# A fused three-layer forward pass on one core: one input tile's layout, one buffer and several places in the order changed

## The chip, the cores and the metric

The kernel runs on one core of one Trainium2 chip. The metric is the device time of one execution in microseconds (us); lower is better.

## What is computed

The input x has 256 rows of 1024 columns, the two memories (mem and mem_2) as many. All is fp32. Cut to what matters:

```python
def first_block(x, mem, ...):
    for l in range(2):
        a = hybrid_mixer(rms_norm(x, pre_mix_g[l]), ...)
        x = x + rms_norm(a, post_mix_g[l])
        c = memory_cross_attention(rms_norm(x, pre_xattn_g[l]), rms_norm(mem, mem_g[l]), ...)
        x = x + rms_norm(c, post_xattn_g[l])
        hdn = jnp.square(jax.nn.relu(rms_norm(x, pre_mlp_g[l]) @ w_up[l]))
        x = x + rms_norm(hdn @ w_down[l], post_mlp_g[l])
    return x

def second_block(x, mem, ...):
    z = rms_norm_2(x, norm_mix_g) @ w_in
    u, v, q, kv, gl = jnp.split(z, splits, axis=-1)
    a = spatial_gating_unit(gelu(u), gelu(v), ...)
    b = nsa_attention(q, kv, gl, ...)
    mixed = concatenate([rms_norm_2(a, mix_out_g[0]), rms_norm_2(b, mix_out_g[1])])
    x = x + mixed @ w_out
    x = x + memory_cross_attention_2(rms_norm_2(x, norm_mem_g), mem, ...)
    return x + square(relu(rms_norm_2(x, norm_ffn_g) @ w_ff1)) @ w_ff2
```

`hybrid_mixer` is one projection into a low-rank query and key-value part (8 heads, rotary part of 32) and a dilated part (8 heads of 64, three window patterns, a position bias), two attentions and one output projection. `memory_cross_attention` has 4 heads of 256. `nsa_attention` joins three branches by a sigmoid gate for each head: a softmax over all earlier keys (the selected blocks are all blocks here, and the window is longer than the input, so both are causal attentions), and one over 15 compressed keys and values. These come from blocks of 32 rows, flattened to 2048 columns, through gelu(flat @ w1 + b1) @ w2 + b2. `memory_cross_attention_2` has 4 heads of 128 with a norm on queries and keys. The MLPs are 4096 wide.

## The kernel before

The 256 rows are two tiles of 128 (t = 0, 1). A fp32 product is made from parts: every operand is split into a hi and a lo part, and three matmuls are summed: hi by hi, hi by lo, lo by hi (`mm3`, L181 to 184).

Weights come in pieces of 512 KB through SP's queue into a ring of four raw buffers, and are split into the ring `whl` of eight: ScalarE writes the hi part (L170, or L174 where a gain is multiplied in), VectorE the lo part (L171, L175). The PSUM banks are four `ps`, two `tp` (mostly transposes), `pf0` and `pf1`.

A normalised and transposed input, `hT`, holds both parts in one tile of shape [128, 2, kt, T] (L308, `new_hT`), part outside, 128-row block of the columns (kt) inside, T = 256. The memory's tile `mem` is made likewise (L507, `load_mem`); hT, the attentions' output `oT` and the like share two buffers under the tag h16. `projA` has the input as the stationary operand and the weights as the moving one. `projS` turns that round, and uses that both parts lie in one tile:

```python
PE.matmul(banks[c], hi[:, cs], xT[2][:, :, k], start=k == 0, stop=False, skip_group_check=True)
PE.matmul(banks[c][:, 0], lo[:, cs], xT[0][:, k], start=False, stop=k == KT - 1, skip_group_check=True)
```

The first (L248) moves 512 columns, hi and lo of the input's block k; the second (L249) 256. `projS` serves the low-rank and dilated projections of the mixer, the memory's keys and, as `up`, the first half of the MLPs.

A scheduler decides the order on each engine from the order in the program and a priority: instructions on VectorE, ScalarE and GpSimd are given one that is 600 earlier (AHEAD, L41). What is to stand inside a projection is handed to it as `at={k: f}`: f is issued ahead of step k. Transposes on TensorE (L278, L405, L628, L826, L902, L1390) are placed so. Such a step needs an operand that VectorE or ScalarE has evacuated from PSUM, and its own result is evacuated by the two in turn.

The places that the change touches:

- Start: twelve matmuls on a constant (L469), and then the gains' transposes.
- `mixer` (L647): key projection, with the transposes of the low-rank inputs (`transp_split(cns[t], ...)` into `cT`) at steps 2 and 5; the rotary key rows `krs`; then the second dilated projection, with the memory's transposes (`memory([0])`) at step 6 and `memory([1])` behind it.
- `mem_attention` (L834), for `cross` (layers 0 and 1, four heads of 256) and `cross2`. A query projection returns a function that transposes it (`turn`). `scores`, softmax and `values` run per row tile; the exps `e` are transposed (L405, result `eT`) and multiplied with the memory's values (L859); L851 are the scores. At its end stand `values(0)`, `turn1()`, `scores(1)`.
- `mlp` (L889): `up01` makes the first two of eight column blocks, with the transposes of the block before (`turn`, L902, of `relu`) at step 3; `down(0)` has the last of them at step 3 too.
- `mixer2` (L1023): projections for u and v with the second row tile's input transposes (`first`) at step 4; pooled and separate keys and values; the first compression layer, `hidden(kd, qs)`, in batches of 16 matmuls of 32 rows by 256 (L1083, kd = 0 for keys, 1 for values), whose weights come through the raw ring; then the query projections with smaller steps inside them. `gates` is a sigmoid from exp. `ckeys0`, `ckeys` make the compressed keys and values, `cscores` their scores. The table `MIX2` (L44) says what is issued ahead of which group of the causal attentions; `mk0`, `mk1` are the second memory's key projection for one row tile each.
- `cross2` (L1367): the query's norms (`head_ms`, four squares with a sum on ScalarE) are read from PSUM in `query`.

## Time and profile before

| | |
|---|---|
| median of three runs | 1209.34 us (1208.45 to 1210.66) |
| profiled execution | 1207.37 us |
| its span, first to last instruction | 1205.3 us |
| TensorE busy (share of the span) | 1178.3 us (98%) |
| VectorE, ScalarE, GpSimd busy | 810.4, 716.5, 83.6 us |
| mean granted TensorE clock | 0.999 |
| share of the chain that ended last | TensorE 76%, DMA 7%, VectorE 7%, ScalarE 6% |
| moved by DMA | 213.12 MB, 177 GB/s on average |

In the rows below PE is TensorE, DVE VectorE, ACT ScalarE, POOL GpSimd, SP the engine whose queue issues the loads. `out<-in` are the tiles an instruction writes and reads, then partitions x elements; xN is a count. A matmul's recorded time overlaps that of the next one, so the price of one is the distance from its start to the next start. The granted clock is the share of TensorE's full clock that the chip allowed. "Idle before <-X" is how long an engine stood ahead of an instruction, and what ended that.

### The profile page before, as it was taken

How to read it: one execution, taken by the hardware profiler on the slowest of the kernel's cores; microseconds unless marked ns; L12 is line 12 of the kernel's file. 1: busy time of each engine (PE TensorE's matmuls, PEld its weight loads, DVE VectorE, ACT ScalarE, POOL GpSimd, SP SyncE). 2: the span in 40 equal slices, each digit the busy share in tenths (PEclk: the TensorE clock that was granted, in tenths of full speed). 3: DMA queues.
4: the chain of work that ended last, by engine and by line, in shares of the span. 5: the costliest groups of instructions: out<-in, count | busy, mean ns of one | idle time of the engine just before them, and what ended most of it. 6: DMA issues, size and time to landing. Idle time of an engine off the chain costs nothing.

```text
span 1205.3 us, 17865 instructions
## 1 busy us (share of the span) xinstructions
PE 1178.3 (98%) x6430; PEld 981.8 (81%) x6430; DVE 810.4 (67%) x1583; ACT 716.5 (59%) x1492; POOL 83.6 (7%) x161
## 2 busy tenths in 40 slices
PE   8999999999999999999999999999999999999998
PEld 6788888888888898778888788887877787888887
DVE  6777766576676676766757676667658657766653
ACT  7766655565565575755648565557676557655551
POOL 1100010110000020000202000002022011000000
PEclk9999999999999999999999999999999999999999
DMA  8856265176656386454625756655663224666560
GB/s 263 296 183 223 98 216 196 59 233 194 191 180 197 116 265 196 148 190 157 208 90 193 240 179 200 195 178 166 198 207 106 88 88 138 211 191 188 183 192 35
DMA packets 92182, 213.12 MB, mean 177 GB/s; under 512 B 7285, under 2 KB 21055, under 8 KB 91327
## 3 DMA queue, kind: packets, MB, share of 16 engines
q1 hardware_dynamic: 91666, 211.62, 54.6%
q8 instruction: 50, 0.82, 0.3%
q10 hardware_dynamic: 428, 0.37, 0.1%
q14 instruction: 38, 0.30, 0.1%
HBM read 205.66 MB, written 6.30 MB: 176 GB/s over the span
## 4 chain that ended last, share of the span: by engine, by line
PE 76%; DMA 7%; DVE 7%; ACT 6%; issue 2%; POOL 1%; SPq 0%; ACTq 0%; POOLq 0%; DVEq 0%
PE ps L184 11%; PE ps L182 11%; PE ps L183 11%; PE pf L248 8%; PE tp L248 6%; PE pf L249 4%; PE pf L182 4%; PE pf L184 4%; PE pf L183 4%; DVE whl L175 3%; PE tp L249 3%; ACT whl L174 2%; DMA raw<-in_w_in_dram 2%; PE ps L446 2%; PE ps L851 1%
## 5 line engine op out<-in xcount | busy, mean ns | idle before, releaser
L175 DVE SCALAR_TENSOR_TENSOR whl<-raw,gT,whl 128x512 fp32r<-128x512 f32 (+5 forms) x416 | 295.0, 750 | 99.1 <-ACT whl L174 98.7
L174 ACT ACTIVATE whl<-raw,gT 128x512 fp32r<-128x512 f32 (+5 forms) x416 | 277.0, 717 | 131.0 <-issue 59.8
L171 DVE TENSOR_TENSOR whl<-raw,whl 128x512 fp32r<-128x512 f32 x264 | 170.3, 686 | 79.6 <-ACT whl L170 79.1
L170 ACT ACTIVATE whl<-raw 128x512 fp32r<-128x512 f32 x264 | 153.7, 628 | 110.7 <-issue 77.7
L182 PE MATMUL ps<-whl,mid 128*128 128x512 f32 x384 | 150.5, 392 | 0.0
L184 PE MATMUL ps<-whl,mid 128*128 128x512 f32 x384 | 149.8, 390 | 0.0
L183 PE MATMUL ps<-whl,mid 128*128 128x512 f32 x384 | 149.6, 390 | 0.0
L248 PE MATMUL pf<-hT,whl 128*128 128x512 f32 x352 | 132.6, 399 | 0.0
L248 PE MATMUL tp<-hT,whl 128*128 128x512 f32 x288 | 107.9, 398 | 0.0
L249 PE MATMUL pf<-hT,whl 128*128 128x256 f32 x352 | 98.8, 281 | 0.0
L182 PE MATMUL ps<-whl,hT 128*128 128x512 f32 (+4 forms) x240 | 85.6, 356 | 0.0
L184 PEld LDWEIGHTS ps<-whl,mid 128*128 128x128 f32 x384 | 72.1, 188 | 15.6
L184 PE MATMUL ps<-whl,hT 128*128 128x512 f32 (+4 forms) x240 | 84.1, 350 | 0.4 <-DVE hT L135 0.4
L182 PEld LDWEIGHTS ps<-whl,mid 128*128 128x128 f32 x384 | 72.1, 188 | 15.1
L183 PE MATMUL ps<-whl,hT 128*128 128x512 f32 (+4 forms) x240 | 84.1, 350 | 0.0
L183 PEld LDWEIGHTS ps<-whl,mid 128*128 128x128 f32 x384 | 72.1, 188 | 14.5
L249 PE MATMUL tp<-hT,whl 128*128 128x256 f32 x288 | 80.9, 281 | 0.0
L248 PEld LDWEIGHTS pf<-hT,whl 128*128 128x128 f32 x352 | 66.1, 188 | 16.2 <-DVE qkd L135 0.3
L249 PEld LDWEIGHTS pf<-hT,whl 128*128 128x128 f32 x352 | 66.5, 189 | 0.0
L248 PEld LDWEIGHTS tp<-hT,whl 128*128 128x128 f32 x288 | 54.1, 188 | 13.2 <-DVE mem L135 0.2
L182 PE MATMUL ps<-whl,oT 128*128 128x512 f32 x152 | 60.8, 400 | 0.0
L184 PE MATMUL ps<-whl,oT 128*128 128x512 f32 x152 | 59.7, 393 | 0.0
(323 smaller groups left out, 2261.9 us busy)
## 6 DMA issues: line engine op xcount, KB each, us to landing
raw<-in_w_up_dram SPq DMA_DIRECT2D x64, 512.0 KB
raw<-in_w_down_dram SPq DMA_DIRECT2D x64, 512.0 KB
raw<-in_w_ff_dram SPq DMA_DIRECT2D x64, 512.0 KB
raw<-in_w_in_dram SPq DMA_DIRECT2D x40, 512.0 KB
raw<-in_w_xk_dram SPq DMA_DIRECT2D x16, 512.0 KB
raw<-in_w_xv_dram SPq DMA_DIRECT2D x16, 512.0 KB
raw<-in_w_mix_out_dram SPq DMA_DIRECT2D x16, 512.0 KB
raw<-in_w_xq_dram SPq DMA_DIRECT2D x16, 512.0 KB
```

What stands on the lines that cost most here:

```text
L170: nc.scalar.activation(hl[:, 0, c:d], raw[:, c:d], AF.Copy)
L171: nc.vector.tensor_tensor(out=hl[:, 1, c:d], in0=raw[:, c:d], in1=hl[:, 0, c:d].bitcast(F32), op=ALU.subtract)
L174: nc.scalar.activation(hi[:, i], r[:, i], AF.Copy, scale=g[i])
L175: nc.vector.scalar_tensor_tensor(lo[:, i], r[:, i], g[i], hi[:, i].bitcast(F32), ALU.mult, ALU.subtract)
L182: PE.matmul(o, sh, mh, start=start, stop=False, skip_group_check=True)
L183: PE.matmul(o, sh, ml, start=False, stop=False, skip_group_check=True)
L184: PE.matmul(o, sl, mh, start=False, stop=stop, skip_group_check=True)
L248: PE.matmul(banks[c], hi[:, cs], xT[2][:, :, k], start=k == 0, stop=False, skip_group_check=True)
L249: PE.matmul(banks[c][:, 0], lo[:, cs], xT[0][:, k], start=False, stop=k == KT - 1, skip_group_check=True)
L446: PE.matmul(cell["o"][j * 64:j * 64 + 64, h // 2], vf(h, kb), pp[j][i][kb] if bias is None else pp[j][i][kb][:, ::-1], start=begin and i = ...
L851: PE.matmul(s[:, i], qT[:, c, tq], kT[:, c], start=(i == 0 and k == 0), stop=k == nkt - 1, skip_group_check=True)
```

## The change

1. hT and mem get the shape [128, kt, 2, T]: for each block k the two parts lie side by side, and L248 moves one run of 512 columns.
2. Fifteen matmuls in place of twelve at the start.
3. First and second mixer layer: cT's transposes at steps 1 and 6. In layer 0 `rows`, `memory([0])` and `memory([1])` go into steps 2, 5 and 7 of the second dilated projection, and `krs` is made behind that.
4. `turn1()` ahead of `values(0)`.
5. MLP: `turn` at step 5 in `up01`, at step 6 in `down(0)`.
6. Second mixer: `first` at step 6; the keys' compression weights in an h16 buffer (`w1`), loaded at the block's start, and their four quarters of `hidden(0)` inside the last pooled projection; `gates` ordered behind the last gelu; compressed keys at steps 1 and 7 of the second query projection, scores inside `mk0`, values inside `mk1`.
7. `cross2`: the query's norms are read from its SBUF copy, and made in `turn`; the last MLP's first weights are converted behind the copy of the last turned query.

```diff
-                PE.matmul(banks[c], hi[:, cs], xT[2][:, :, k], start=k == 0, stop=False, skip_group_check=True)
+                PE.matmul(banks[c], hi[:, cs], xT[2][:, k], start=k == 0, stop=False, skip_group_check=True)
...
-        h = h16p.tile([128, 2, kt, T], F32R, tag="h16", name=nm)
-        return (h[:, 0], h[:, 1], h)
+        h = h16p.tile([128, kt, 2, T], F32R, tag="h16", name=nm)
+        return (h[:, :, 0], h[:, :, 1], h)
...
-    for _ in range(12):
+    for _ in range(15):
...
-        memT[2] = memp.tile([128, 2, 8, T], F32R, tag="mem", name="mem")
-        memT[0], memT[1] = memT[2][:, 0], memT[2][:, 1]
+        memT[2] = memp.tile([128, 8, 2, T], F32R, tag="mem", name="mem")
+        memT[0], memT[1] = memT[2][:, :, 0], memT[2][:, :, 1]
...
-                                    at={2 + 3 * t: lambda t=t: transp_split(cns[t], t, cT, 0, 5) for t in range(2)})):
+                                    at={1 + 5 * t: lambda t=t: transp_split(cns[t], t, cT, 0, 5) for t in range(2)})):
...
-            rows()
             memory = load_mem(I["mem"])
+        wd = load_all(w, 8, 1184, 512, gp)
+        for i, b in enumerate(projS(wd, hT, 4, ["ps", "ps", "pf0", "pf1"], at={2: rows, 5: lambda: memory([0]), 7: lambda: memory([1])} if l == 0 else {})):
+            halves(qkd[:, 1, i], b)
...
-        wd = load_all(w, 8, 1184, 512, gp)
-        for i, b in enumerate(projS(wd, hT, 4, ["ps", "ps", "pf0", "pf1"], at={6: lambda: memory([0])} if l == 0 else {})):
-            halves(qkd[:, 1, i], b)
...
-            memory([1])
...
+        turn1()
         values(0)
-        turn1()
         scores(1)
...
-            ws = [load_all(w_up, 8, j * 512, 512, g) for j in range(2)]
+            if held[0] is None:
+                ws = [load_all(w_up, 8, j * 512, 512, g) for j in range(2)]
+            else:
+                with tc.issue_after(held[0].ins):
+                    ws = [load_all(w_up, 8, j * 512, 512, g) for j in range(2)]
...
-                    at = {} if turn is None else {3: turn}
+                    at = {} if turn is None else {5: turn}
...
-            last = down(j, mids, {} if j else {3: turn})
+            last = down(j, mids, {} if j else {6: turn})
...
-            uvb = [projA(wuv[i], hT, t, [(0, 512)], at={4: first} if i == 1 and t == 0 else {})[0] for i in range(2)]
+            uvb = [projA(wuv[i], hT, t, [(0, 512)], at={6: first} if i == 1 and t == 0 else {})[0] for i in range(2)]
...
+        w1 = h16p.tile([128, 16, 256], F32, tag="h16", name="w1")
+        for q4 in range(4):
+            nc.sync.dma_start(w1[:, q4 * 4:q4 * 4 + 4],
+                              I["cmp_w1_2"][0, 0, q4 * 512:q4 * 512 + 512, :].rearrange("(m p) n -> p m n", p=128))
...
-            wib[t], = projA(ww, hT, t, [(0, 280)])
+            wib[t], = projA(ww, hT, t, [(0, 280)], at={2 * q + 1: lambda q=q: hidden(0, [q]) for q in range(4)} if t else {})
             keys(t)
-            if t == 0:
-                hidden(0)
...
-            for t in range(2):
-                A.activation(gate[:, t].rearrange("p h b -> p (h b)"), wib[t][:, 256:280], AF.Exp, scale=-1.0)
+            with tc.issue_after(cell["gelu"].ins):
+                for t in range(2):
+                    A.activation(gate[:, t].rearrange("p h b -> p (h b)"), wib[t][:, 256:280], AF.Exp, scale=-1.0)
...
-        queries(1, projA(wq, hT, 1, [(0, 512)], "pf0", at={0: lambda: hidden(1, [2]), 2: lambda: hidden(1, [3]),
+        queries(1, projA(wq, hT, 1, [(0, 512)], "pf0", at={0: lambda: hidden(1, [2]), 1: ckeys, 2: lambda: hidden(1, [3]),
                                                            3: lambda: keysT(1), 4: lambda: queriesT(0),
-                                                           5: lambda: (strips(1), gates()), 6: gateT})[0])
+                                                           5: lambda: (strips(1), gates()), 6: gateT, 7: ckeysT})[0])
...
-               "mk0": lambda: mk(0), "mk1": lambda: mk(1, cscores()), "mkn": mkn,
+               "mk0": lambda: mk(0, cscores()), "mk1": lambda: mk(1, {1: cvalues}), "mkn": mkn,
```

What it moves, at three places. First TensorE in layer 0's memory attention, from the transposes of `e` (L405) to the scores (before L859 are the values, L826 the query's transposes, L851 the scores; in the change their lines are 858, 825 and 850). Before:

```order
L405 MATMUL tp<-cm,e 128x128 [waits DVE_49]
L405 MATMUL tp<-cm,e 128x128
L859 MATMUL ps<-eT,xv 128x128 [waits DMAHW3_49,Activation_49]
L859 MATMUL ps<-eT,xv 128x128 x7
L859 MATMUL ps<-eT,xv 128x128 [waits DVE_49]
L859 MATMUL ps<-eT,xv 128x128 x7
L826 MATMUL tp<-cm,sc 128x128 [waits PE_49]
L826 MATMUL tp<-cm,sc 128x128 x3
...
L851 MATMUL ps<-xkT,qT 128x256 [waits Activation_49]
L851 MATMUL ps<-xkT,qT 128x256 x3
```

Now:

```order
L825 MATMUL tp<-cm,sc 128x128 [waits Activation_49]
L825 MATMUL tp<-cm,sc 128x128 x3
L825 MATMUL tp<-cm,sc 128x128 [waits DVE_49]
L825 MATMUL tp<-cm,sc 128x128 x3
L405 MATMUL tp<-cm,e 128x128 [waits Activation_49]
L405 MATMUL tp<-cm,e 128x128 x3
L405 MATMUL tp<-cm,e 128x128 [waits DVE_49]
L858 MATMUL ps<-eT,xv 128x128 [waits DMAHW3_49,Activation_49]
L858 MATMUL ps<-eT,xv 128x128 x7
L405 MATMUL tp<-cm,e 128x128 x3
L858 MATMUL ps<-eT,xv 128x128 [waits DVE_49]
L858 MATMUL ps<-eT,xv 128x128 x7
L850 MATMUL ps<-xkT,qT 128x256 x8
```

The query's transposes now open the piece and wait for its evacuation by ScalarE and then VectorE. The turning of `e` is cut into four, one and three, and the second half of the values comes behind the last three.

Second ScalarE in the second mixer, around the compression's gelu (`hc`), the gates (`small`) and the exps of the first causal group (`e`); ACT_TABLE_LOAD brings a function's table in. Before:

```order
L135 ACT_TABLE_LOAD
L135 ACTIVATE small<-ps 128x24
...
L135 ACTIVATE small<-ps 128x24
L135 ACT_TABLE_LOAD
L135 ACTIVATE hc<-hp,gT_99 128x30 [waits DVE_49]
L135 ACTIVATE hc<-hp,gT_99 128x30
...
L135 ACTIVATE scf<-pf_8360 128x512 [waits DVE_49]
L174 ACTIVATE whl<-raw,gT_99 128x1024 [waits DMAHW4_49]
L135 ACT_TABLE_LOAD [waits DVE_49]
L135 ACTIVATE e,den<-ps,sm,small 128x128 [waits PE_49]
```

Now:

```order
L135 ACTIVATE hc<-hp,gT_99 128x30 [waits DVE_49]
L135 ACTIVATE hc<-hp,gT_99 128x30
L135 ACT_TABLE_LOAD
L135 ACTIVATE small<-ps 128x24 x2
L135 ACTIVATE vw<-tp 128x512 [waits PE_49]
L135 ACTIVATE nx<-tp,gqk 128x30 [waits PE_49]
...
L135 ACTIVATE scf<-pf_8361 128x512 [waits DVE_49]
L174 ACTIVATE whl<-raw,gT_99 128x1024 [waits DMAHW2_49]
L174 ACTIVATE whl<-raw,gT_99 128x1024 [waits DMAHW3_49]
L135 ACTIVATE e,den<-ps,sm,small 128x128 [waits DVE_49,PE_49,Pool_49]
```

The gates' exps are behind all gelus; one table load is left of three, and none stands ahead of `e`.

Third ScalarE in the second memory attention, from the evacuation of the last query (`sc`) to that of its transposes (`qT`); L174 are conversions of the last MLP's weights. Before:

```order
L174 ACTIVATE whl<-raw,gT_99 128x512 [waits DMAHW6_49,PE_49]
L174 ACTIVATE whl<-raw,gT_99 128x512
L135 ACTIVATE sc<-pf_9443 128x256 [waits PE_49]
L135 ACTIVATE eT<-tp 128x512 [waits PE_49]
L174 ACTIVATE whl<-raw,gT_99 128x512 [waits DMAHW7_49]
L135 ACTIVATE junk,sm<-pf_9443 128x128 [waits DVE_49]
L174 ACTIVATE whl<-raw,gT_99 128x512
L135 ACTIVATE junk,sm<-pf_9443 128x128 [waits Activation_49]
L135 ACTIVATE oT<-ps 128x2x128 [waits PE_49]
L135 ACTIVATE junk,sm<-pf_9443 128x128 [waits Activation_49]
L135 ACTIVATE oT<-ps 128x2x128 [waits PE_49]
L135 ACTIVATE junk,sm<-pf_9443 128x128 [waits Activation_49]
L135 ACTIVATE qT<-tp 128x4x128 [waits PE_49]
```

Now:

```order
L135 ACTIVATE sc<-pf_9443 128x256 [waits PE_49]
L135 ACTIVATE junk,sm<-sc 128x128 [waits Activation_49] x2
L135 ACTIVATE junk,sm<-sc 128x128 [waits DVE_49,Activation_49]
L135 ACTIVATE qT<-tp 128x4x128 [waits PE_49]
L135 ACTIVATE junk,sm<-sc 128x128 [waits Activation_49]
L174 ACTIVATE whl<-raw,gT_99 128x512 [waits DMAHW5_49]
L174 ACTIVATE whl<-raw,gT_99 128x512
L135 ACTIVATE oT<-ps 128x2x128 [waits PE_49]
L135 ACTIVATE eT<-tp 128x512 [waits PE_49]
L174 ACTIVATE whl<-raw,gT_99 128x512 [waits DMAHW6_49]
L174 ACTIVATE whl<-raw,gT_99 128x512
L135 ACTIVATE oT<-ps 128x2x128 [waits PE_49]
```

The turned query's evacuation passes the conversions and the evacuations of `eT` and `oT`; the four squares read the copy, and two conversions stand ahead of `oT` and `eT`.

## Rows read from the trace of the kernel before

**Rows 1.** The page: its first line, and part 1, the row of TensorE.
```profile
span 1205.3 us, 17865 instructions
...
PE 1178.3 (98%) x6430; PEld 981.8 (81%) x6430; DVE 810.4 (67%) x1583; ACT 716.5 (59%) x1492; POOL 83.6 (7%) x161
```

**Rows 2.** Waits of TensorE: result waited for, releaser: total us, number, longest us.
```profile
PE tp L902 <- DVE relu L135: 2.1, 4, 1.1
PE ps L851 <- ACT qT L135: 1.9, 3, 1.3
PE ps L859 <- ACT eT L135: 1.8, 3, 1.3
PE tp L405 <- DVE e L135: 1.7, 2, 1.6
PE tp L628 <- DVE cT L135: 1.4, 1, 1.4
PE pf L1083 <- DMA raw<-in_cmp_w_dram: 1.3, 1, 1.3
PE tp L278 <- DVE cT L135: 1.2, 1, 1.2
```

**Rows 3.** Groups by line and shape, TensorE: count, busy us, mean ns of one.
```profile
L183 PE MATMUL ps<-whl,mid 128*128 128x512 f32 x384 | 149.6, 390 | 0.0
L248 PE MATMUL pf<-hT,whl 128*128 128x512 f32 x352 | 132.6, 399 | 0.0
```

**Rows 4.** Order of time on TensorE, three stretches: start us, duration us, line, form.
```profile
857.08 0.28 PE L184 MATMUL ps<-whl,hT 128*128 128x256 f32 x1
...
865.38 0.28 PE L184 MATMUL ps<-whl,hT 128*128 128x256 f32 x1
...
1048.88 0.40 PE L182 MATMUL ps<-whl,mid 128*128 128x512 f32 x1
...
1056.39 0.39 PE L182 MATMUL ps<-whl,mid 128*128 128x512 f32 x1
...
1057.07 0.39 PE L248 MATMUL tp<-hT,whl 128*128 128x512 f32 x1
...
1068.36 0.40 PE L182 MATMUL ps<-whl,mid 128*128 128x512 f32 x1
```

**Rows 5.** Order of time on TensorE, the warm-up.
```profile
0.95 4.77 PE L469 MATMUL pf<-mhalf 128*32 128x512 bf16 x12 [0.95 <-POOL mhalf L135]
```

**Rows 6.** Order of time on VectorE, first mixer; in brackets idle before and releaser.
```profile
53.66 0.49 DVE L135 TENSOR_SCALAR scf<-sc,smf 128x512 f32<-128x512 f32 x1 [1.48 <-POOL smf L135]
```

**Rows 7.** Order of time on TensorE, layer 0's memory attention (L405 turns e).
```profile
204.33 3.84 PE L859 MATMUL ps<-eT,xv 128*128 128x128 f32 x32 [0.25 <-ACT eT L135]
208.01 1.04 PE L826 MATMUL tp<-cm,sc 128*128 128x128 f32 x8
209.35 0.48 PE L851 MATMUL ps<-xkT,qT 128*128 128x256 f32 x1 [0.30 <-ACT qT L135]
```

**Rows 8.** Order of time on ScalarE, then VectorE, same place: second query's copies.
```profile
202.94 0.58 ACT L135 ACTIVATE sc<-pf 128x512 f32<-128x512 f32 x1
...
203.60 0.68 DVE L135 TENSOR_SCALAR sc<-pf 128x512 f32<-128x512 f32 x1
```

**Rows 9.** Order of time on TensorE, start of the second mixer.
```profile
838.39 1.06 PE L278 MATMUL tp<-cm,sc 128*128 128x128 f32 x8 [0.55 <-DVE sc L135]
```

**Rows 10.** Order of time on ScalarE, second mixer and second memory attention.
```profile
899.76 1.28 ACT L135 ACT_TABLE_LOAD   x1
...
997.30 2.57 ACT L174 ACTIVATE whl<-raw,gT 128x512 fp32r<-128x512 f32 x4
```

**Rows 11.** Windows: us, busy us (count) of each engine, granted clock (PEclk), DMA.
```profile
904.00:919.80 15.80, 13.45 (x88) 10.57 (x87) 12.09 (x37) 12.38 (x43) 4.91 (x7) 1.00 0.39 134
919.80:923.30 3.50, 3.50 (x24) 2.73 (x24) 3.03 (x10) 0.66 (x3) 0.00 (x0) 0.51 0.00 0
995.00:1007.00 12.00, 9.40 (x56) 7.95 (x55) 10.97 (x23) 10.23 (x28) 1.73 (x4) 1.00 0.76 244
```

More of the change, by code (lines that the diff above doesn't have):

```diff
@@ L43 @@
 AHEAD = 600
[L44 removed]
+MIX2 = {1: "gating mk0", 2: "mk1 norm0", 3: "norm1 first0 cprobs", 4: "finish0 mkn first1 rn0", 5: "mv0",
         6: "out0"}
@@ L335, in body @@
     evac_flip = [0]
+    held = [None]
     def copy_any(o, i):
@@ new lines, in mixer2, with ckeys @@
+        vr = tp[:, 256:512].rearrange("p (k h g n) -> p k h g n", k=2, h=2, g=4)
+        vbk = nx[:, 0, 256:768].rearrange("p (h d) -> p h d", h=8)
+        es = nx[:, 0, 0:256]
+        G.memset(es, 0.0)
+        def ckeys():
+            kcb = ps([30, 64], "tp")
+            for hf in range(2):
+                PE.matmul(kcb, hc[:, 0, hf], w2[:, 0, hf], start=hf == 0, stop=False,
+                          skip_group_check=True)
+            PE.matmul(kcb, ones1[0:1, 0:30], b2[:, 0:64], start=False, stop=True, skip_group_check=True)
+            kc = tp[0:30, 0:128]
+            sq = tp[0:30, 160:224]
+            ms = sm(16)
+            A.activation(sq, kcb, AF.Square, scale=0.125, accum_out=ms[0:30, 0:1])
+            a = sm(16)
+            V.tensor_scalar(a[0:30, 0:1], ms[0:30, 0:1], EPS, None, ALU.add)
+            r = sm(16)
+            G.tensor_tensor(out=r[0:30, 0:1], in0=a[0:30, 0:1], in1=mhalf[0:30, 0:1], op=ALU.pow)
+            for i in range(2):
+                V.tensor_scalar(kc[:, i * 64:i * 64 + 64], kcb, r[0:30, 0:1], None, ALU.mult)
@@ L1295, in weigh @@
                 V.tensor_tensor(out=e15, in0=e15, in1=dn.unsqueeze(2).to_broadcast([128, 16, 15]), op=ALU.mult)
-            return {2 * t + h + 1: lambda t=t, h=h: some(t, h) for t in range(2) for h in range(2)}
+            return {2 * t + h + 2: lambda t=t, h=h: some(t, h) for t in range(2) for h in range(2)}
         def cprobs():
```

90 lines of the change are left out of this document (36 added, 54 removed).

## Prediction

> **What bounds the kernel now.** I read the page first: TensorE is busy 1178.3 of 1205.3 us, 98% of the span, and stands for the other 27.0, while VectorE and ScalarE have a third of theirs free [rows 1]. So only two things can move the end: what a matmul costs from the start of one to the start of the next, and the few us in which TensorE stands. The profiled execution took 1207.37 us, 2.07 more than its span and 1.97 under the median of 1209.34; I make the sum as a difference and take it from both. Second, the list of TensorE's waits: nearly all are short and for an evacuation by VectorE or ScalarE, one is for a DMA [rows 2]. The edits aim at these one by one. Third, the groups by shape and the order of time in three stretches without a wait, for the price of one matmul [rows 3, 4]. Last, the places of the waits in order of time.
>
> **Input parts side by side.** L248 multiplies one weight tile with both parts of the input, 512 columns. Before, these are two runs of 1 KB that lie 8 KB apart; now they are one run of 2 KB. It stands 832 times in the program (704 with the normalised input, 128 with the memory), each followed by a 256-column L249. From 1057.07 to 1068.36 there are 32 such pairs: 352.8 ns a pair [rows 4]. The same shapes with plain operands: 33 matmuls of 512 columns in 7.51 us, 227.6 ns; 69 of 256 columns in 8.30 us, 120.3 ns [rows 4]. Together 347.9, so a pair costs 4.9 ns more than its two parts do elsewhere. I take this as the price of the second run: 832 x 4.9 ns = 4.1 us gained. The low end is nothing, if the surplus comes from the alternation of sizes, which stays. The high end is by the recorded durations, 399 against 390 ns [rows 3]: 832 x 9 ns = 7.5 us.
>
> A rule speaks against this. The Trainium skill (SBUF — State Buffer, Specifications) says that SBUF has 16-byte lines and that each cross to a new line costs something; two runs of 1 KB cross as many lines as one of 2 KB but for one, and by that rule this part is worth nothing; the rows have a surplus, but don't name its cause.
>
> **Three more warm-up matmuls.** Twelve took 4.77 us [rows 5], so three more are at most 1.2 us, ahead of everything. The stretch behind them waits for evacuations and for the input, which absorbs most. I take +0.3; ends 0 and +1.2.
>
> **First mixer.** The transposes of the low-rank inputs move from steps 2 and 5 to 1 and 6 of the key projection, the memory's into steps 5 and 7 of the next. The waits aimed at are 1.4 and 1.2 us [rows 2]. But the 1.4 has its root elsewhere: VectorE itself stood 1.48 us until 53.66 for a result of GpSimd, and everything it evacuates is behind that [rows 6]. TensorE now gets past the transposes, and stands a little later, when the next projection wants bank pf0, which VectorE empties behind the same wait. I take -0.5; ends 0 and -2.6. The rotary key rows (GpSimd fills and VectorE sums) come later, and nobody waits for them before the attention: nothing, or at the worst the 0.7 us of one more evacuation.
>
> **Query turn ahead of the values, layers 0 and 1.** This I expect to cost. Before, the order is: turn e (covered), wait 0.25, values for 3.84 us, turn the query (1.04), wait 0.30, scores [rows 7]. During the values the query's copies were long done. Now the query is turned first, right behind its own projection, which ends about where turning e began: 204.33 less 0.25 and 1.04, near 203.05. ScalarE's half of the query's copy ends at 203.52 and VectorE's at 204.28 [rows 8]: TensorE idles some 0.5 us to the first, then turns four (half of 1.04), idles 0.2, turns four, to 204.8. e has no bank until ScalarE has copied the turned half, 0.58 us [rows 8] behind one conversion: to about 204.9. Four of e, then the fifth waits for VectorE's copy, 0.68 behind two conversions of 0.68: to about 206.1, 0.7 idle. First half of the values, 1.9, to 208.1; three of e; VectorE's copy, 0.8 idle; second half to 211.2. There the scores start, before at 209.35: +1.9 us. A conversion more or less on either engine moves that by 0.6, so I take +1.6 a layer, **+3.2** for two. Ends: +4 and -1.1, the latter if the two waits of both layers simply vanish.
>
> **MLP.** Four waits of the transposes at L902 for relu sum to 2.1 us [rows 2]; the two edits put them two and three steps (0.68 us each, three matmuls of 227.6 ns) later, more than the longest wait of 1.1. They carry nothing but a later mid, which is read after the projection. -2.1; ends 0 and -2.1.
>
> **Second mixer's start.** The transposes go from step 4 to 6 and the wait of 0.55 before them [rows 9] with them: -0.5; ends 0 and -0.55.
>
> **First compression weights.** The batch at L1083 waited 1.3 us for its DMA [rows 2], as the ring of four raw buffers was full. Now it has a buffer of its own and is loaded at the start of the block, and its four pieces stand inside a projection. The loads pass the pooled projection's on SP's queue, but no other DMA holds TensorE up here; if that cover goes, 1.3 us comes back for another load. The four pieces interrupt the projection four times in place of once. -1.0; ends 0 and -1.3.
>
> **Gates, compressed keys, scores and values.** Exps and gelus alternated on ScalarE, with a table load of 1.28 us at 899.76 just ahead of the exps of the first group [rows 10]; in the new order there is one load before the gates and the two others are gone. The transposes of e waited 1.6 us for those exps [rows 2]. The compressed scores move from the second key projection into the first, one step apart, and the keys' chain into the query projection, six steps apart. -1.6, and +0.4 back, as the key projection starts on a bank that the query's copy frees (one copy is 0.58 [rows 8]): **-1.2**; ends 0 and -2.1, the other small waits included.
>
> **Clock.** From 919.8 to 923.3 the granted clock was 0.51, 1.2 in place of 2.4 GHz, in 3.50 us of work; at full clock that takes half, so the spell cost 1.7 us. TensorE had been busy 13.45 of the 15.80 us ahead of it [rows 11]. With the wait of 1.6 gone and larger matmuls in this stretch I take -1.7; ends 0 and -1.7.
>
> **Second memory attention.** Both waits are 1.3 us [rows 2]. ScalarE converted MLP weights for 2.57 us, and the query's copy stood behind them [rows 10]. Now these wait for the turned query. But the norms of the query (four short reads) stand ahead of its second copy, and two conversions ahead of e's: by the same walk the scores start 0.5 to 1 us sooner. -0.7; ends 0 and -2.6. The weights are wanted only after an output projection and a norm, which hide their later start; without that cover the 2.57 us of conversions come back.
>
> **Sum:** -4.1 + 0.3 - 0.5 + 3.2 - 2.1 - 0.5 - 1.0 - 1.2 - 1.7 - 0.7 = -8.3 us. The profiled execution would take 1199.1, the median **1201.0**.
>
> **Rivals.**
> *The layout is worth nothing* (the line rule above gives this too). Then -4.2: 1205.1. For it: the plain stretches are each of one size, so no row shows what the change of size from matmul to matmul costs. Against: the longer recorded durations [rows 3] are those of L248 itself.
> *The waits go and none comes back.* The turn costs nothing and the second memory attention gives its 2.6: -8.3 - 3.2 - 1.9 - 1.6 = -15, 1194. For it: VectorE and ScalarE have a third of their time free. Against: both convert weights in just these stretches.
> *The clock falls in the emptied crossings: slower.* With the query turn first, TensorE works some 6 of the 8.2 us from 203.05 to 211.2 (1.04 for the turn, as much for e, 3.84 for the values), a smaller share than ahead of the drop at 919.8, a third of it on small transposes. A us at the lower clock loses half a us; it takes 2 x (8.3 + 2.4) = 21 us of lower clock over the three crossings, 7 each, to make the kernel slower by 2.4. With 10 each the loss is 15, and the time 1216. Against it: from 995 to 1007 TensorE was busy only 9.40 of 12.00 us, and the clock stayed at 1.00 [rows 11].
>
> **Chances.** The forecast, with sizes off by some us, 0.50; layout nothing 0.27; all waits gone 0.17; slower 0.06. 0.2%, 2.4 us, is what a measurement of this kernel tells from no change. Of the layout rival, at -4.2, a fifth ends within it, and of the forecast a twentieth: same 0.08, faster 0.86, slower 0.06. The range reaches down past most of the third case and up past the layout rival with the clock's 1.7 not gained: 1191 to 1207.
>
> **What would show it.** Right: pairs at 348 ns a pair; no wait at L902 over 0.2; no DMA wait at the compression; one table load between 870 and 905; no lower clock after 900; in layers 0 and 1 waits of 0.5 to 0.8 at the query's turns and at e, and scores 1.5 to 2 us later after the projection. Wrong: pairs still at 353 (layout nothing); no new waits in the crossings (third case); a granted clock of 0.5 in them (slower); or new waits of over 1 us for pf0 in the first mixer or for MLP weights at the end.

## The result: slower by 0.8%

The change takes 1219.09 us (median of 6 runs, 1217.01 to 1220.55) where the kernel before takes 1209.42 beside it (6 runs, 1207.53 to 1210.66): a ratio of 1.008 with a 95% interval from 1.0065 to 1.0095, 9.7 us slower. Forecast were 1201.0, 1191 to 1207. The profiled execution of the change took 1220.18 us, 1.1 over its median; that of before lies 2.05 under the median of these runs, so the two traces differ by 12.8 us, 3.1 more than the medians do. The granted clock was 0.999 in that execution of before, and 0.996 on average in the 111 executions of before that stand beside the experiments below; 0.003 of the span is 3.6 us.

The page of the change, its first line, busy time and chain:

```profile
span 1218.3 us, 17858 instructions
...
PE 1183.2 (97%) x6433; PEld 982.4 (81%) x6433; DVE 810.9 (67%) x1583; ACT 713.2 (59%) x1490; POOL 83.4 (7%) x161
...
PE 81%; ACT 6%; DMA 5%; DVE 5%; issue 2%; POOL 1%; SPq 0%; ACTq 0%; DVEq 0%; POOLq 0%
```

Against [rows 1] the span is 13.0 us longer. TensorE is busy 4.9 us more and stands 8.1 us more (35.1 against 27.0). The three more matmuls of the start are at most 1.2 us of that (12 took 4.77, [rows 5]); more busy time for otherwise the same matmuls means that some ran at a lower clock. First the waits of TensorE (columns as in [rows 2]):

```profile
PE tp L278 <- DVE eT L135: 3.4, 1, 3.4
PE ps L446 <- ACT eT L135: 2.8, 2, 2.1
PE pf L248 <- DVE qkd L135: 2.2, 1, 2.2
...
PE ps L184 <- DVE hT L135: 1.8, 1, 1.8
PE tp L405 <- ACT qT L135: 1.6, 3, 0.7
PE ps L858 <- DVE eT L135: 1.6, 2, 0.8
...
PE ps L436 <- DVE qkd L135: 1.4, 1, 1.4
PE ps L182 <- ACT relu L135: 1.4, 1, 1.4
PE ps L858 <- ACT eT L135: 1.1, 3, 0.7
...
PE tp L901 <- DVE relu L135: 0.2, 1, 0.2
```

Nearly every wait that the change aimed at is gone, as forecast: no DMA at the compression, no `cT`, and L901 (L902 before) at 0.2 where [rows 2] had 2.1. Others stand in their place, and the two longest are new. The places in order of time on TensorE:

```profile
55.53 0.50 PE L248 MATMUL pf<-hT,whl 128*128 128x512 f32 x1 [2.16 <-DVE qkd L135]
...
71.28 0.82 PE L436 MATMUL ps<-qkd 64*128 64x128 f32 x8 [1.45 <-DVE qkd L135]
...
206.25 1.42 PE L825 MATMUL tp<-cm,sc 128*128 128x128 f32 x8 [0.37 <-ACT sc L135]
208.08 0.65 PE L405 MATMUL tp<-cm,e 128*128 128x128 f32 x4 [0.41 <-ACT qT L135]
208.92 0.33 PE L405 MATMUL tp<-cm,e 128*128 128x128 f32 x1 [0.19 <-DVE qT L135]
209.42 2.05 PE L858 MATMUL ps<-eT,xv 128*128 128x128 f32 x16 [0.17 <-ACT eT L135]
...
212.58 2.05 PE L858 MATMUL ps<-eT,xv 128*128 128x128 f32 x16 [0.78 <-DVE eT L135]
...
678.09 0.50 PE L182 MATMUL ps<-whl,mid 128*128 128x512 f32 x1 [0.73 <-ACT mid L135]
...
680.85 0.50 PE L182 MATMUL ps<-whl,mid 128*128 128x512 f32 x1 [1.36 <-ACT relu L135]
...
853.60 0.50 PE L184 MATMUL ps<-whl,hT 128*128 128x512 f32 x1 [1.80 <-DVE hT L135]
...
931.57 0.63 PE L278 MATMUL tp<-cm,sc 128*128 128x128 f32 x4 [3.35 <-DVE eT L135]
934.30 1.97 PE L446 MATMUL ps<-eT,vw 128*64 128x128 f32 x16 [2.11 <-ACT eT L135]
...
1070.07 0.39 PE L248 MATMUL tp<-hT,whl 128*128 128x512 f32 x1
...
1081.36 0.40 PE L182 MATMUL ps<-whl,mid 128*128 128x512 f32 x1
```

And the windows of the change (columns as in [rows 11]):

```profile
10.70:14.00 3.30, 3.12 (x7) 2.51 (x8) 3.30 (x6) 2.74 (x7) 0.00 (x0) 0.53 0.70 222
206.00:217.00 11.00, 9.09 (x60) 7.68 (x61) 6.03 (x10) 3.63 (x7) 0.00 (x0) 1.00 0.58 200
853.80:857.10 3.30, 3.30 (x9) 2.59 (x9) 1.49 (x4) 1.68 (x4) 0.00 (x0) 0.52 0.87 265
920.00:931.50 11.50, 8.21 (x50) 6.54 (x48) 9.94 (x21) 6.96 (x22) 1.22 (x2) 1.00 0.42 138
934.30:939.00 4.70, 4.70 (x27) 3.14 (x28) 2.70 (x12) 2.81 (x11) 1.22 (x2) 0.50 0.45 157
```

Right behind the wait of 1.80, and behind those of 3.35 and 2.11, the granted clock is 0.52 and 0.50, 1.2 GHz, with TensorE at work all the time: 3.30 and 4.70 us of work that take half of it at full clock, some 1.7 and 2.4 us lost beside the waits. A third spell lies at the start (10.7 to 14.0, 0.53); 13 of the 15 kernels with twelve warm-up matmuls have one there too in their traces, so it is not the longer warm-up's. In the trace of before there is one spell [rows 11].

The start of each stage's first matmul in both traces, and the difference of their distances, show where the time comes from ("x" is the memory attention):

| stretch | before, us | change, us | difference |
|---|---|---|---|
| start to the memory projection of layer 0 | 71.62 | 72.03 | +0.41 |
| memory projection, layer 0 | 39.19 | 41.41 | +2.22 |
| x scores to output projection, layer 0 | 19.94 | 22.28 | +2.34 |
| MLP layer 0, first up projection | 36.03 | 35.47 | -0.56 |
| x scores to output projection, layer 1 | 19.94 | 22.37 | +2.43 |
| MLP layer 1, first up projection | 37.66 | 38.99 | +1.33 |
| second mixer to its memory keys | 68.31 | 72.78 | +4.47 |
| memory keys to output projection | 27.43 | 29.53 | +2.10 |
| second x, scores to output projection | 16.37 | 15.49 | -0.88 |
| MLP of the last block, first up projection | 36.07 | 35.47 | -0.60 |
| all other stretches together | | | -0.26 |

### The profile page after: what moved, and what is told of

The parts are those of the page before. It is cut to its first block, busy times and chain, and to the rows that moved or that the text cites. A ratio compares the mean times of both kernels' runs of the same rounds, so it can differ in the third digit from the quotient of the medians.

```text
span 1218.3 us, 17858 instructions
## 1 busy us (share of the span) xinstructions
PE 1183.2 (97%) x6433; PEld 982.4 (81%) x6433; DVE 810.9 (67%) x1583; ACT 713.2 (59%) x1490; POOL 83.4 (7%) x161
## 4 chain that ended last, share of the span: by engine, by line
PE 81%; ACT 6%; DMA 5%; DVE 5%; issue 2%; POOL 1%; SPq 0%; ACTq 0%; DVEq 0%; POOLq 0%
PE ps L182 12%; PE ps L184 12%; PE ps L183 12%; PE pf L248 8%; PE tp L248 6%; PE pf L182 4%; PE pf L184 4%; PE pf L183 4%; PE pf L249 4%; PE tp L249 3%; ACT whl L174 2%; DVE whl L175 2%; PE ps L436 2%; PE ps L446 2%; DMA raw<-in_w_in_dram 2%
## 5 line engine op out<-in xcount | busy, mean ns | idle before, releaser
L174 ACT ACTIVATE whl<-raw,gT 128x512 fp32r<-128x512 f32 (+5 forms) x416 | 277.2, 717 | 137.7 <-issue 68.6
L248 PE MATMUL pf<-hT,whl 128*128 128x512 f32 x352 | 133.0, 400 | 2.3 <-DVE qkd L135 2.2
L248 PE MATMUL tp<-hT,whl 128*128 128x512 f32 x288 | 108.0, 398 | 0.0
L248 PEld LDWEIGHTS pf<-hT,whl 128*128 128x128 f32 x352 | 66.1, 188 | 19.0 <-DVE qkd L135 3.1
L248 PEld LDWEIGHTS tp<-hT,whl 128*128 128x128 f32 x288 | 54.1, 188 | 13.3 <-DVE mem L135 0.2
```

The lines of the kernel that those rows point to most:

```text
L174: nc.scalar.activation(hi[:, i], r[:, i], AF.Copy, scale=g[i])
L248: PE.matmul(banks[c], hi[:, cs], xT[2][:, k], start=k == 0, stop=False, skip_group_check=True)
```

## Experiments

The stretches above are what each trace is read by. A ratio stands with its 95% interval, against runs of the kernel before on the same chip. The span and the mean granted clock of every execution were taken, too. Span times (1 - clock) is an estimate of what an execution lost to the lower clock, which counts each us at half the clock as half lost, though TensorE stands for some of them. The executions of before lost 4.5 to 5.2 us on average in the four sets beside the experiments, and the six of the change 7.1: of the change's 9.7 us some 2 are lower clock, and some 7 are not. Below, "by the clock" is this estimate against the runs of before beside it.

### The input's layout (e1_layout, e8_sorted)

e1_layout has the layout alone; the order on every engine is that of before.

```diff
-        h = h16p.tile([128, 2, kt, T], F32R, tag="h16", name=nm)
+        h = h16p.tile([128, kt, 2, T], F32R, tag="h16", name=nm)
...
-                PE.matmul(banks[c], hi[:, cs], xT[2][:, :, k], start=k == 0, stop=False, skip_group_check=True)
+                PE.matmul(banks[c], hi[:, cs], xT[2][:, k], start=k == 0, stop=False, skip_group_check=True)
```

> The kernel before with the new layout of hT and mem alone; the order on every engine is that of the kernel before. Theory (two full runs cost no more than one, the surplus of a pair is the change of size): a pair of L248 and L249 stays at 353 ns, the time within 1 us of before. Rival (the second run costs, and the change's other parts hide the gain): a pair at 348 ns, the time 4 us lower.

Measured: 1209.21 us, 0.9998 [0.9986, 1.0010]. The 32 pairs of e1_layout in order of time on TensorE:

```profile
1059.00 0.39 PE L248 MATMUL tp<-hT,whl 128*128 128x512 f32 x1
...
1070.29 0.40 PE L182 MATMUL ps<-whl,mid 128*128 128x512 f32 x1
```

11.29 us, 352.8 ns a pair, to the digit what [rows 4] give; and the change itself has the same 11.29 (1070.07 to 1081.36, above). The layout is worth nothing. The line rule of the Trainium skill (SBUF — State Buffer, Specifications) gave that, and the trace agrees: 0.0 ns a pair. What then are the 4.9 ns? e8_sorted keeps the old layout and groups the matmuls of a step by size.

```diff
                 PE.matmul(banks[c], hi[:, cs], xT[2][:, :, k], start=k == 0, stop=False, skip_group_check=True)
+            for c in range(nch):
+                cs = slice(c * 128, c * 128 + 128)
                 PE.matmul(banks[c][:, 0], lo[:, cs], xT[0][:, k], start=False, stop=k == KT - 1, skip_group_check=True)
```

> The kernel before with the matmuls of one step of projS in the order of their sizes: first the 512-column ones of all banks, then the 256-column ones. Theory (the surplus of a pair is the change of size): a step of four banks costs 4 x 227.6 + 4 x 120.3 = 1392 ns plus a change or two in place of 1411 ns, 208 steps: 2.5 to 4 us less of TensorE's time. Rival (the surplus belongs to the 512-column matmul on this operand whatever stands beside it): a step at 1411 ns, no gain.

Measured: 1208.93 us, 0.9985 [0.9967, 1.0002]. The same 32 pairs in e8_sorted, order of time on TensorE:

```profile
1056.19 0.62 PE L248 MATMUL tp<-hT,whl 128*128 128x512 f32 x2
...
1067.39 0.40 PE L182 MATMUL ps<-whl,mid 128*128 128x512 f32 x1
```

11.20 us, 350.0 ns a pair: 2.8 of the 4.9 ns go with the alternation of sizes; what the other 2.1 are no run shows. By the ratio the whole kernel gains some 1.8 us, and the interval just touches no change.

### The query's turn (e2_turn, e9_turn_cross2, e11_change_no_turn)

```diff
-        values(0)
         turn1()
+        values(0)
         scores(1)
```

> The kernel before with the query's turn ahead of the values alone (layers 0 and 1 and the second memory attention). Theory (TensorE waits for the query's copies): from the first scores to the output projection 2.3 us more in each of layers 0 and 1, 0 to 1 us more in the second memory attention, in all 4.5 to 6 us slower. Rival (the extra waits stand only because the earlier parts of the change shifted the conversions into that place): under 1.5 us.

Measured: 1216.78 us, 1.0056 [1.0039, 1.0073], from four executions, of which the profiled one, 1221.93, is the slowest. Layers 0 and 1 lose 2.27 and 2.43 us, as in the change. The second memory attention, which runs the same lines, loses 4.93 more in this trace. Windows of e2_turn there:

```profile
1013.00:1020.00 7.00, 6.31 (x23) 5.29 (x23) 3.40 (x7) 2.53 (x8) 1.92 (x4) 0.50 0.69 205
```

Its turn waited 1.72 us for the query's copy behind the weight conversions, `e` 1.28 for the turned query, and during that second wait the clock halved. e9_turn_cross2 is e2_turn with the change's edit of the second memory attention (norms read the copy, weights wait for the turned query).

> The kernel before with the query's turn ahead of the values and with the second memory attention's own edit (norms from the copy and in the turn, MLP weights behind the last turned query's copy). Theory (the 4.9 us that the turn alone cost in the second memory attention come from conversions ahead of the query's copy and a clock drop, and its own edit takes these away): 2.3 us more in each of layers 0 and 1, -0.5 to 0.5 in the second memory attention, in all 4 to 5 us slower. Rival (the second memory attention loses by the turn in any case): 7 us slower or more.

Measured: 1213.66 us, 1.0031 [1.0017, 1.0045]; layers 0 and 1 +2.39 and +2.45, the second attention 0.86 *shorter* than before, and no low clock in it. Between these two traces that edit is worth 5.8 us where the turn stands first; between the ratios of the two kernels 0.25%, some 3 us. The trace of e2_turn holds this spell, and its granted clock of 0.991 is below that of the three other executions (0.993 to 0.998). Without the turn the edit is worth 1.7 (e14_sum below). e11_change_no_turn is the change with `values(0)` back ahead of `turn1()`.

> The changed kernel with the values ahead of the query's turn again, as before, in all three attentions. Theory (the costs of the parts add): 4.7 us less than the changed kernel from layers 0 and 1, and 0 to 1 us from the second memory attention: 1213 to 1215 us, 0.3 to 0.5% slower than before. Rival (the parts don't add, and the turn is only one way to lose the same time): over 1217.

Measured: 1215.06 us, 1.0042 [1.0027, 1.0056], by the ratios 0.38% or some 4.6 us less than the change. The turn costs about the same among the other edits as in the two layers of e2_turn (2.27 + 2.43), and about half of the loss is something else.

### Gates and compressed keys (e4_gates, e10_scores_back)

e4_gates has the reordering of gates, compressed keys, scores and values alone:

```diff
-MIX2 = {1: "gating ckeys0 mk0 ckeys", 2: "mk1 norm0", ...
+MIX2 = {1: "gating mk0", 2: "mk1 norm0", ...
...
-               "mk0": lambda: mk(0), "mk1": lambda: mk(1, cscores()), "mkn": mkn,
+               "mk0": lambda: mk(0, cscores()), "mk1": lambda: mk(1, {1: cvalues}), "mkn": mkn,
```

> The kernel before with the reordering of gates, compressed keys, scores and values alone. Theory (the exps of the second group of heads stand on ScalarE behind a conversion that waits for its load, the turn of eT waits, and the clock drops): a wait of 2 to 3.5 us for eT between mk1 and the output projection, granted clock near 0.5 for 3.4 or 6.8 us there, 2 to 4 us slower. Rival (this wait comes from the later loads through the early compression weights): no such wait, 2 us faster.

Measured: 1212.48 us, 1.0026 [1.0015, 1.0038]. Waits of TensorE in e4_gates:

```profile
PE tp L278 <- DVE eT L135: 3.4, 1, 3.4
...
PE ps L446 <- ACT eT L135: 2.6, 2, 1.8
```

The two longest waits of the change are there with this edit alone. Why, ScalarE of the change shows, in order of time:

```profile
904.04 1.28 ACT L135 ACT_TABLE_LOAD   x1
...
928.91 1.33 ACT L174 ACTIVATE whl<-raw,gT 128x512 fp32r<-128x512 f32 x2 [1.82 <-DMA raw<-in_w_mkv_dram]
930.15 0.44 ACT L135 ACTIVATE e<-ps,sm,small 128x128 f32<-128x128 f32 x1
...
933.20 0.47 ACT L135 ACTIVATE e<-ps,sm,small 128x128 f32<-128x128 f32 x1
933.63 0.61 ACT L135 ACTIVATE eT<-tp 128x512 f32<-128x512 f32 x1
```

One table load, as forecast. But the causal scores of the second head group are in PSUM by 920.7, and their exps start at 930.15: VectorE reaches the reduction that they need at 927.44, behind three conversions of 1.28 us and shorter work, and ScalarE first converts a weight whose load came late. In the kernel before, the compressed scores (L1273) stood in this very place, order of time on TensorE:

```profile
914.81 1.95 PE L1273 MATMUL pf<-nx,kq 64*128 64x15 f32 x16
...
918.06 2.00 PE L1273 MATMUL tp<-nx,kq 64*128 64x15 f32 x16
919.99 1.97 PE L446 MATMUL ps<-eT,vw 128*64 128x128 f32 x16
```

3.95 us of small matmuls, behind which L446 did not wait at all. The edit has moved them ahead of the chain's start, where they cover nothing. By the clock 1.8 us of what e4_gates loses is lower clock, and some 1 us is not. e10_scores_back is e4_gates with the scores back in the second key projection:

```diff
-               "mk0": lambda: mk(0, cscores()), "mk1": lambda: mk(1, {1: cvalues}), "mkn": mkn,
+               "mk0": lambda: mk(0), "mk1": lambda: mk(1, {1: cvalues, **cscores()}), "mkn": mkn,
```

> The reordering of gates and compressed keys alone (as in e4), but with the compressed scores left inside mk1, behind the second group's scores. Theory (the compressed scores, 32 small matmuls, were TensorE's work while ScalarE and VectorE finish the second group's exps, and in front of that group they cover nothing): the wait for eT ahead of the output projection goes from 3.4 to under 1 us, no clock drop there, 2 to 4 us less than e4, so 1 us slower to 1 us faster than before. Rival (ScalarE stands behind a weight load in any order): the wait stays over 2 us, the time that of e4.

Measured: 1214.27 us, 1.0035 [1.0021, 1.0049], no better. The wait is gone (L278 for `eT`: 0.2), so its cause is shown. The time is still lost: windows of e10_scores_back,

```profile
912.00:922.00 10.00, 10.00 (x34) 7.97 (x35) 4.26 (x17) 3.27 (x9) 0.00 (x0) 0.52 0.35 105
```

10 us of work at a clock of 0.52, 4.8 us lost where before lost 1.7 [rows 11]; later comes another spell. Without the difference of 3.1 the stretch from the memory keys to the output projection (+1.45) would be some 1.7 us shorter than before, an estimate. All ten executions say the same: by the clock e10_scores_back loses 4.3 us more than before, and without it takes as long (0.1 more). Why the clock fell for longer here no run settles.

Nor does a spell at this place come with the edit alone. Windows of e1_layout and e5_mix0, which leave this stretch as before:

```profile
905.00:935.00 30.00, 27.82 (x186) 21.08 (x184) 25.40 (x75) 20.31 (x70) 6.12 (x9) 1.00 0.34 107
905.00:935.00 30.00, 28.44 (x161) 21.99 (x160) 24.14 (x69) 20.89 (x76) 6.13 (x9) 0.89 0.26 88
```

Of the twelve traces with the old order here (that of before among them), the clock over these 30 us is 1.00 in four, 0.94 in two and 0.89 in six; with the moved scores, in e4_gates, it is 0.89. The spell of [rows 11] is thus an execution's, and no fixed part of the order. But on average the reordering makes it worse: the four kernels that have it, alone or beside other edits (e4_gates, e10_scores_back, e11_change_no_turn, e12_best), lose 1.8 to 5.3 us more by the clock than before, clear of noise.

### First mixer (e5_mix0, e13_mix0_ct)

e5_mix0 has the first mixer's moves alone; e13_mix0_ct the same with the transposes of `cT` at steps 2 and 5, as before.

```diff
-                                    at={2 + 3 * t: lambda t=t: transp_split(cns[t], t, cT, 0, 5) for t in range(2)})):
+                                    at={1 + 5 * t: lambda t=t: transp_split(cns[t], t, cT, 0, 5) for t in range(2)})):
...
+        for i, b in enumerate(projS(wd, hT, 4, ["ps", "ps", "pf0", "pf1"], at={2: rows, 5: lambda: memory([0]), 7: lambda: memory([1])} ...
```

> The kernel before with the moves in the first mixer alone (cT's transposes at steps 1 and 6, rows and the memory's transposes inside the second dilated projection, krs behind it). Theory (the waits for cT come back as a wait for bank pf0, and the memory's second transposes no longer cover the copies of qkd): no wait at cT, but one of about 2 us at L248 for qkd and two of 0.7 to 1.5 us at the memory's transposes and at the first L436; by the start of the cT projection 1.5 to 2.5 us slower, as much in all. Rival (these waits only fill with what the earlier parts shifted): within 0.5 us of before.

> The first mixer's moves as in e5, but with cT's transposes at steps 2 and 5 as before. Theory (VectorE stands for GpSimd's smf until 53.5, and TensorE meets that either at cT or, once past it, at bank pf0): the wait at L628 for cT is back at 1 to 1.5 us, the wait of L248 for qkd falls from 2.4 to under 1 us, and the time is within 1 us of e5, as the two are one wait. Rival (the moved transposes of cT are themselves the cost): 2 us less than e5.

Measured: e5_mix0 1212.84 us, 1.003 [1.0013, 1.0046]; e13_mix0_ct 1211.74, 1.0011 [0.9996, 1.0026]. Waits of TensorE in e5_mix0:

```profile
PE pf L248 <- DVE qkd L135: 2.8, 2, 2.4
...
PE ps L436 <- DVE qkd L135: 1.3, 1, 1.3
...
PE tp L405 <- DVE e L135: 1.2, 3, 0.8
```

The memory projection is 2.24 us longer in e5_mix0 and 2.23 in e13_mix0_ct (2.22 in the change), so this difference does not come from the steps of `cT`. It is what stands inside it: with the memory's transposes pulled into the second dilated projection, only 8 of 18 score matmuls (L436) stand ahead of the memory projection. Not all of it is lost: the matmuls that moved in take some 0.7 of it, and ahead of it they are missing. The largest piece is the first eight transposes of `e`, in e5_mix0 and then in the kernel before:

```profile
91.25 0.94 PE L405 MATMUL tp<-cm,e 128*128 128x128 f32 x4
92.44 1.02 PE L405 MATMUL tp<-cm,e 128*128 128x128 f32 x4 [0.25 <-DVE e L135]
...
95.33 1.09 PE L405 MATMUL tp<-cm,e 128*128 128x128 f32 x8
```

From the first of them to the next projection matmul they take 2.11 us in place of 0.85, with gaps and a wait between them. Ahead of the projection e13_mix0_ct is 1.66 us earlier than e5_mix0, its wait split between `cT` (0.9) and pf0 (1.6) in place of 2.4 at pf0 and a spell of lower clock. By the ten executions of each, both lose 1.5 to 1.6 us without the lower clock, and the lower clock adds 1.6 in e5_mix0 and nothing in e13_mix0_ct; the intervals overlap, so whether the steps of `cT` bring that clock stays open.

### Second mixer's start (e3_w1, e6_first6, e7_w1_first6)

e3_w1 has the compression weights' buffer and the four pieces in the projection, e6_first6 the later step, e7_w1_first6 both.

```diff
-            uvb = [projA(wuv[i], hT, t, [(0, 512)], at={4: first} if i == 1 and t == 0 else {})[0] for i in range(2)]
+            uvb = [projA(wuv[i], hT, t, [(0, 512)], at={6: first} if i == 1 and t == 0 else {})[0] for i in range(2)]
```

> The kernel before with the compression weights in their own buffer, loaded at the block's start, and its quarters inside the projection. Theory (the four early loads share the DMA engines with the last load of the u and v weights, ScalarE stands behind that load, the norm and the transposes of the second row tile come late, and the clock drops once): the L174 pair at the start of the second mixer waits 2.5 to 3 us in place of 0.6, TensorE's waits at the transposes and hT grow by 2 us or more, 2 to 4 us slower from the second mixer's start to mk, in spite of the 1.3 us saved at the compression. Rival (the stage is lost by the reordering of gates and compressed keys or by step 6): 1 us faster.

> The kernel before with the second row tile's transposes at step 6 in place of 4 at the start of the second mixer, alone. Theory (two steps less to evacuate hT in, and VectorE has two operations on uv first): the wait at the transposes shrinks by up to 0.5 us, the waits for hT behind them grow to 1.5 to 2.2 us; from the second mixer's start to mk 1 to 2 us slower, and up to 1.7 more if the clock drops. Rival (the 4.5 us lost there are the early weight loads' alone): 0.5 us faster.

> The early compression weights and the transposes at step 6 together. Theory (the two act on the same wait, as the late norm and the short cover add): from the second mixer's start to mk 3 to 4.5 us more than before, with a clock drop at 850 us. Rival (each for itself, w1 alone having shown nothing): the sum of the two alone, within 0.5 us.

Measured: e3_w1 1208.7 us, 0.9996 [0.9984, 1.0009]; e6_first6 1211.51, 1.0009 [0.9996, 1.0022]; e7_w1_first6 1211.34, 1.0003 [0.9987, 1.0020]. None can be told from no change. But the wait is there: e6_first6, order of time on TensorE,

```profile
845.48 0.50 PE L184 MATMUL ps<-whl,hT 128*128 128x512 f32 x1 [1.80 <-DVE hT L135]
```

and 1.79 in e7_w1_first6: two steps later the transposes have two steps less between them and the projection that reads them. In the profile of e6_first6 the clock then falls (0.57 from 846.5 to 850.5) and the stretch to the memory keys is 2.30 us longer; in that of e7_w1_first6 it does not, and the stretch is 0.64 longer. The wait stands in all four traces with step 6 (1.80, 1.79, 1.79 in e11_change_no_turn, 1.80 in the change); the spell comes in three of them.

### Can the parts be put together better? (e12_best, e14_sum, e15_sum_mlp1)

All three start from the kernel before, with e8_sorted's order and the change's edits of the second memory attention and the MLPs. e12_best adds e3_w1 and e10_scores_back; e14_sum adds nothing; e15_sum_mlp1 is e14_sum with layer 1's MLP left as before:

```diff
-                    at = {} if turn is None else {5: turn}
+                    at = {} if turn is None else {3 if extra else 5: turn}
...
-            last = down(j, mids, {} if j else {6: turn})
+            last = down(j, mids, {} if j else {3 if extra else 6: turn})
```

> The kernel before with projS in the order of sizes, the early compression weights, the second memory attention's edit, the MLP's later turns, and the gates as in e10; without the turn ahead of the values, the first mixer's moves, step 6, the new layout and the longer warm-up. Theory (costs and gains add): sizes -2, compression weights -0.5 to -1, second memory attention -0.5 to -2, MLP -1, gates 0: 4 to 7 us faster than before, 1203 to 1206. Rival (every gain returns as a wait elsewhere): within 2 us of before.

> The kernel before with projS in the order of sizes, the second memory attention's edit and the MLP's later turns alone. Theory (what e12 lost, it lost in the second mixer by the reordered gates and the clock drops that go with them): sizes -1.5 to -2.5, second memory attention -1.7, MLP -0.6, +0.5 and -0.6: 2.5 to 5 us faster than before. Rival (the gains come back as waits wherever TensorE runs ahead): within 1.5 us of before.

> As e14, but layer 1's MLP keeps its turns at step 3. Theory (in that MLP the memory's load sets the up weights back, ScalarE waits for them ahead of the turned block's copy, and two steps later that copy is behind one wait more): layer 1's up01 at the time of the kernel before within 0.7 us, in place of 1.1 to 1.3 us more, 0.5 to 1 us less than e14. Rival (the 1.3 us are the spread of loads from run to run): the same as e14.

Measured: e12_best 1212.42 us, 1.002 [1.0009, 1.0030], slower; e14_sum 1207.45, 0.9972 [0.9959, 0.9984]; e15_sum_mlp1 1205.95, **0.9946 [0.9927, 0.9966]**, faster than both kernels (its medians give 0.9963). e12_best loses 6.4 us in the second mixer, in its trace with low clock (0.68 to 0.85 in three stretches of 10 us): by the clock it loses 5.3 us more than before, and without that it would be 2.7 faster. e14_sum, order of time on TensorE, second memory attention:

```profile
1001.52 2.05 PE L861 MATMUL ps<-eT,kv 128*128 128x128 f32 x16 [0.52 <-ACT eT L135]
...
1004.69 1.56 PE L853 MATMUL ps<-kv,qT 128*128 128x256 f32 x6 [0.69 <-ACT qT L135]
```

Two waits of 1.3 before are 0.52 and 0.69, and the stretch is 1.74 us shorter. Its first MLP stretches are -0.57, +0.79 and -0.61. In the one trace of e15_sum_mlp1 layer 1's was +2.59, with two waits for VectorE's `relu` (0.69 and 2.05) and a spell behind the second, so the step that was put back does not explain its lead. The single executions say more: without the lower clock e14_sum and e15_sum_mlp1 are 3.3 and 3.5 us faster than before, the same, and the lead is in the clock (0.5 more and 1.4 less lost than before), too near the noise to be the edit's. This stretch moved between -0.09 and +1.71 us in kernels that leave the MLPs alone: what the edit does in layer 1 stays open.

## Why the prediction was wrong, step by step

The sign failed at one habit of the sum: it priced the waits that each edit takes away, and put what the moved work had covered, or would now stand behind, at nothing or near it (only +3.2 for the turn and +0.4 for the gates). The runs show new waits of 1.4 to 3.4 us in three of the edited stages (first mixer, start of the second, gates), and more time at the lower clock behind the gates. Two of its own signs of being wrong came: pairs at 353 ns, and over 1 us of waiting for pf0.

- **Input side by side, -4.1: nothing.** The step that failed is "I take this as the price of the second run". The surplus of 4.9 ns was there, but it was read against stretches that differ in two things, the run and the alternation; e8_sorted gives 2.8 of it to the alternation. The layout rival had it right, with 0.27. (The plain stretch of 256 columns in [rows 4] has four transposes of 128 columns inside; ahead of them 41 matmuls take 119.9 ns each, so the price stands.)
- **Gates, -1.2, and clock, -1.7: +3.1 for e4_gates** (its median over that of before is +2.76, its last matmul +3.13 later in the trace). I priced the waits that the edit removes, and took +0.4 for what comes back. I did not ask what the 32 moved matmuls had covered where they stood. The waits of 3.35 and 2.11 are the answer. The clock term had a second fault: it took the spell of one execution for a part of the order, and in the traces of other kernels the same order has none, as long a one or a longer one. In the change a spell came behind those waits.
- **Query's turn, +3.2: +4.8** (2.34 and 2.43). The mechanism and the order of the waits (0.37, 0.41, 0.19, 0.17, 0.78) are those walked through. The size of the term failed: from the first of the query's transposes to the first of `e` it took 1.83 us (206.25 to 208.08), where the walk gave some 1.4; the first values came late by about as much, and I had rounded the walk's own 1.9 down to 1.6.
- **First mixer, -0.5: about +2 in the trace, +3.1 for e5_mix0 by its medians.** That the wait returns at pf0 was right (2.16). Missed was what the moves do around the memory projection: a new wait of 1.45 at the first scores, and `e` turned in 2.1 us in place of 0.9. By the clock about half of what e5_mix0 loses on average is lower clock.
- **Second mixer's start, -0.5: a new wait of 1.8**, and in three of four traces a spell behind it (1.7). The step counted the wait ahead of the transposes, and not the shorter way to their reader. The two make 3.5 of the 4.47 us that the change loses from the second mixer's start to the memory keys; the rest no run assigns.
- **MLP, -2.1: -0.57, +1.33, -0.61.** Two of three blocks gained some 0.6. In layer 1 the waits came back at `mid` (0.73) and `relu` (1.36), behind a weight conversion whose load was late; +1.33 is within what this stretch moves in kernels without the edit.
- **Compression weights, -1.0: not measurable** (e3_w1, -0.5 by the ratio, the interval on both sides of none), though the wait of 1.3 for the DMA is gone. **Second memory attention, -0.7: -0.88**, as forecast (-1.74 where the turn does not stand first). **Warm-up, +0.3:** the first projection begins 1.07 later and 0.53 of it is made up; with twelve warm-ups e5_mix0 and e6_first6 have +0.96 and +0.94, so it is not the warm-ups'.

The slower rival had the right sign and the wrong place. In layers 0 and 1 the clock stayed at 1.00 (the window from 206 to 217) with 9.09 of 11 us busy. It fell in the second mixer of the change and in the second attention of e2_turn. Parts alone, by ratios: turn with the attention's edit +0.31%, first mixer +0.30, gates +0.26, step 6 +0.09, layout and weights -0.06 together: +0.9% against +0.8 measured (the MLPs' edits were not run alone), so the parts add up within their intervals.

## What to carry to other kernels

Before moving small work away from a place, ask which chain ran beside it there: cover shows in no list of waits until it is gone, and here 3.95 us of small matmuls, once moved, came back as waits of 3.4 and 2.1. A surplus per instruction is priced only against a stretch that differs in one thing. And judge each edit alone and against several runs, since one trace may hold a spell of lower clock that another execution lacks; the granted clock of each execution, read beside its time, told the waits' share of a loss from the clock's.

## What was unexpected of the chip

The granted clock falls to half in spells of 3 to 10 us, in a kernel whose TensorE is 97% busy. Leaving out the first 20 us and the last 10, the 17 traces have 22 of them. Ten begin during or within 2 us after a TensorE wait of 1.7 us or more, and two behind one of 1.6; the other ten begin between 912 and 926, in the second mixer, with no wait of 1 us in the 8 us ahead. Nor does each such wait bring one: 1.79 us in e7_w1_first6 had none, and after 2.16 us at 55.53 the change ran on at full clock. A spell costs half its length: behind the wait of 1.80 us as much again, 1.7. And 512- and 256-column matmuls in turn cost 352.8 ns a pair, grouped by size 350.0.
